# Moving 64 of 256 tokens out of the dense expert scans into gathers by index

## The chip, the core and the metric

The kernel runs on one core of a Trainium2 chip. The metric is the device time of one execution in microseconds. Work is done by TensorE (PE, with its weight loads shown as PEld), VectorE (DVE), ScalarE (ACT) and GpSimd (POOL); SyncE (SP) issues most transfers. Each engine works through its own queue in order and waits for the others by semaphores.

## The reference

The reference is a network of two layers of a first kind (three sequence mixers, then a routed feed-forward part) and two of a second kind (mixing, cross-attention, feed-forward), on 256 tokens of 1024 features. The change concerns the routed part, `peer_ffn`, which is computed once per layer of the first kind. For each token 8 heads pick 16 of 16384 experts each, by product keys:

```
q = (xt @ w_query).reshape(T, H, 2, PEER_HALF)
s = jnp.einsum('thcd,cnd->thcn', q, sub_keys)
sv, si = lax.top_k(s, K)
cand_s = (sv[:, :, 0, :, None] + sv[:, :, 1, None, :]).reshape(T, H, K * K)
cand_i = (si[:, :, 0, :, None] * PEER_NKEYS + si[:, :, 1, None, :]).reshape(T, H, K * K)
top_s, pos = lax.top_k(cand_s, K)
idx = jnp.take_along_axis(cand_i, pos, axis=-1)
gate = jax.nn.softmax(top_s, axis=-1)
a = jnp.einsum('thkd,td->thk', down[ib], xb)
c = gb * jax.nn.gelu(a)
out = jnp.einsum('thk,thkd->td', c, up[ib])
```

So a token needs 128 rows of `down` and 128 rows of `up`, each of 1024 values.

## The kernel before

`peer` does not gather. It computes the product of every token with every one of the 16384 experts, multiplies the result by a mask that holds the gate where the token picked the expert and zero elsewhere, and multiplies that by the whole `up` table. Both tables are read once per layer, in 128 tiles of 128 experts each (512 KB). There are four runs of 64 tiles, in this order: `dscan(0, ga[0])` (here the first down scan), `dscan(1, ga[1])` (the second down scan), `uscan(0)` (the first up scan) and `uscan(1)` (the second up scan).

Every weight tile goes through `wt` (line 248). SP loads it into one of four buffers `wr`; ACT rounds it to a high part `wh` (line 255), DVE subtracts that from the tile to get a low part `wl` (line 256), four buffers each. `mm3` (line 301) then does three products for each 128x128 piece: high by high (line 303), high by low (304), low by high (305), in the type fp32r, with new weights for each. A tile has 8 pieces, hence 24 products; the moving side is 128 features (or experts) by 256 tokens. In a down scan the products of two tiles are summed in PSUM (`col`) and ACT writes their GELU into `ga` (line 1179). In an up scan the moving side is the masked result, split into `xh` and `xl` by `coef` (line 1353, by way of lines 293 and 294), and all 256 experts' halves sum into four PSUM tiles `acc`.

Two helpers run beside the scans and put their instructions between the tiles. `routing()` picks the experts during the first down scan. `build(half, dst)` makes the masks, 8 tokens at a time: DVE writes one-hot rows (lines 1314 and 1329), PE multiplies them (line 1338, f16), DVE multiplies the mask into `ga` (line 1320). `build(0)` runs beside the second down scan and `build(1)` beside the first up scan, 32 blocks each.

How much of a helper stands between two tiles is set by credit. `tick` (line 267), called once by each `wt`, adds a rate to the credit (`R1` to `R3`: 1150, 1500, 1600) and takes steps of the helper as long as the credit is above zero; each step says its cost as it yields. `H1 = H2 = 0` ties the helper's DVE instructions behind the latest `wl`. `drain` runs a helper to its end. The second up scan has no helper.

Of the kernel before, what the change touches and what calls it, by code (L numbers as in the profile page):

```python
# [23 lines left out]
F32 = mybir.dt.float32  # L24
# [3 lines left out]
U32 = mybir.dt.uint32  # L28
AF = mybir.ActivationFunctionType
OP = mybir.AluOpType  # L30
# [90 lines left out]
def prep(inp):  # L121
# [11 lines left out]
    for l in range(DEPTH):  # L133
# [14 lines left out]
        a[f"sk{l}"] = bd  # L148
        a[f"down{l}"] = np.ascontiguousarray(
            i["peer_down"][l].reshape(128, 128, 8, 128).transpose(0, 3, 2, 1)).reshape(128, 128, 1024)  # L150
        a[f"up{l}"] = np.ascontiguousarray(i["peer_up"][l]).reshape(128, 128, 1024)

        w = i["w_in_2"][l]
# [44 lines left out]
class K:  # L198
    def __init__(self, ctx, tc, ap, ahead):
        self.tc, self.nc, self.ap, self.ctx = tc, tc.nc, ap, ctx  # L200
        nc = self.nc
        self.P = ctx.enter_context(tc.tile_pool(name="keep", bufs=1))
        self.W = ctx.enter_context(tc.tile_pool(name="wts", bufs=1))
        self.S = ctx.enter_context(tc.tile_pool(name="scr", bufs=1))
        self.ps = ctx.enter_context(tc.tile_pool(name="psum", bufs=1, space=PSUM))
        self.dr = ctx.enter_context(tc.tile_pool(name="dram", bufs=1, space=DRAM))
        self.x = self.P.tile([128, 8, T], F32, name="xres", bufs=1)
        self.nw = self.P.tile([128, 13, 8], F32, name="nw")
        self.eps = self.P.tile([128, 1], F32, name="eps")
# [20 lines left out]
        self.todo, self.sqs = [], []  # L230

    def cap(self, name, rows=128):
        o, w = _COFF[name]
# [31 lines left out]


    def tick(self):
        self.credit += self.rate
        while self.side is not None and self.credit > 0:
            try:  # L270
                cost = next(self.side)
                if cost is None:
                    break
                self.credit -= cost
            except StopIteration:
                self.side = None
        if self.side is None:
            self.credit = 0.0
# [131 lines left out]
    def tail(self, accs, rows, wi, scale=None):  # L410

        self.pre(wi)
        if wi == N_FIN:
# [5 lines left out]
        def done(d):  # L419
            s = slice(2 * d, 2 * d + 2)  # L420
            xs = self.x[:, s]
            if scale is None:
# [11 lines left out]
        self.lastrows(accs, rows, done)  # L434
        if wi != N_FIN:
            self.todo = self.norm_steps()
            return
# [38 lines left out]
    def colpair(self, srcs, xh, xl):  # L476
# [4 lines left out]
        else:  # L481
            for j, s in enumerate(srcs):
                h, l = self.wt(s)
                self.coltile(ps[:, j], h, l, xh, xl)
        return ps

    def cols(self, W, c0, n, xh, xl, evac):
# [625 lines left out]
WARM = 14  # L1113
R1, R2, R3 = 1150, 1500, 1600
H1 = H2 = 0


def peer(k, l, nxt):
# [4 lines left out]
    with k.tc.tile_pool(name=f"peer_{l}", bufs=1) as p:  # L1123
# [5 lines left out]
        ga1 = p.tile([128, HI * T], F32, name="ga1")  # L1129
        top = ExitStack()  # L1130
        q = top.enter_context(k.tc.tile_pool(name=f"first_{l}", bufs=1))
        ga = [q.tile([128, HI * T], F32, name="ga0"), ga1]

        rt, off = ga[1], [HI * T - 13000]

        def rtile(*shape):
            n = 1
# [1 line left out]
                n *= s  # L1139
            a = rt[:, off[0]:off[0] + n]  # L1140
            off[0] += n
            assert off[0] <= HI * T
# [12 lines left out]
        nc.sync.dma_start(sk, ap[f"sk{l}"])  # L1155
        k.cols(ap[f"w_q{l}"], 0, 8, xh, xl, lambda j, m, ps: V.tensor_mul(qT[:, j:j + m], ps, k.rsb))

        for h in range(0, 8, 2):
            for tt in range(2):
                ps = k.pst("mx", [128, 2, 256])  # L1160
                for j in range(2):
                    nc.tensor.matmul(ps[:, j], qT[:, h + j, tt * 128:(tt + 1) * 128], sk, start=True, stop=True)  # L1162
                c = h + tt
                t = k.S.tile([128, 2, T], F32, name="sq", bufs=2)[:, 0]
                V.scalar_tensor_tensor(t, k.x[:, c], k.nw[:, N_FFN + l, c:c + 1], k.rs, op0=OP.mult, op1=OP.mult)
                k.split(xh[:, c], xl[:, c], t)
                nc.scalar.copy(sc[:, tt, h:h + 2], ps)
        TB = 8
        room = k.P.tile([128, 4096], F16, name="xres", bufs=1)
        sizes = (TB * 128, TB * HI, 2 * TB * HI)  # L1170
# [5 lines left out]

        def dscan(half, dst):
            def ev(j, m, ps):
                nc.scalar.activation(dst[:, j * T:(j + m) * T], ps[:, :m].rearrange("p a t -> p (a t)"), AF.Gelu_apprx_tanh)  # L1179
            k.cols(down, half * HI, HI, xh, xl, ev)  # L1180


        sv = rtile(2, 8, 2, 16)
# [14 lines left out]
        def routing():  # L1198
# [79 lines left out]
            for src, kind in ((ij[0], 0), (ij[1], 1), (gt, 2)):  # L1278
# [8 lines left out]
                else:  # L1287
# [3 lines left out]
                    V.tensor_copy(g3[:, :, 0], gb)  # L1291
                    V.tensor_sub(g3[:, :, 1], gb, g3[:, :, 0])

        k.beside(routing(), R1, H1)
        dscan(0, ga[0])

        sets = [[room[:, starts[i]:starts[i + 1]] for i in range(3)],
                [k.S.tile([128, sizes[0]], F16, name="sq", bufs=2), room[:, starts[3] + sizes[0]:starts[3] + sizes[0] + sizes[1]],
# [1 line left out]
        pairs = io16.rearrange("p (a d) -> p a d", d=2)  # L1300

        def build(half, dst):
            d3 = dst.rearrange("p (i t) -> p i t", t=T)
            hs = slice(half * HI, (half + 1) * HI)

            def parts(b):
# [37 lines left out]
        dscan(1, ga[1])  # L1344
        k.drain()
        accs = k.rows_begin()
        ring = [k.S.tile([128, 8, T], F32R, name=n, bufs=1) for n in ("xh", "xl")]
        end = []

        def at(i):  # L1350
            return [t[:, i % 8] for t in ring] if i < 2 * HI - 2 else [t[:, i % 2] for t in end]

        def coef(i):
            r, o = i % 8, i % HI * T
            h, lo = [t[:, r:r + 2] for t in ring] if i < 2 * HI - 2 else end
            k.split(h.rearrange("p a t -> p (a t)"), lo.rearrange("p a t -> p (a t)"), ga[i // HI][:, o:o + 2 * T])

        def uscan(half):
            for i in range(half * HI, (half + 1) * HI, 2):
# [2 lines left out]
                if i % HI + 2 < HI:  # L1362
                    coef(i + 2)
                if i == 2 * HI - 2:
                    k.tail(accs, [k.wt(ap[f"up{l}"][e]) + tuple(at(e)) for e in (i, i + 1)], nxt, scale=1.0 / GS)
# [399 lines left out]
```

## Time and profile before

| | us |
|---|---|
| three runs, median | 2915.08 |
| lowest and highest of them | 2913.3, 2918.97 |
| the profiled execution | 2919.18 |
| its span | 2917.1 |
| PE busy in it | 2889.8 |
| DVE busy | 2077.0 |
| ACT busy | 1457.7 |

The span runs from the first to the last instruction of the profiled execution. An engine's busy time is the time in which at least one of its instructions was under way; PE's includes the run-out of pipelined products, so what a product costs is read from the distance between two starts.

### The profile page before, as it was taken

The numbers are of one execution on the slowest core, as the hardware profiler recorded it, in microseconds if no ns is written. First come the engines' busy times: TensorE is split into PE (matmuls) and PEld (weight loads), VectorE is DVE, ScalarE is ACT, GpSimd is POOL, SyncE is SP. The second block draws the span as 40 slices with busy tenths as digits, with TensorE's granted clock in tenths as the row PEclk, the third lists the DMA queues.
The fourth block names the chain that finished last, engine by engine and source line by source line (L and its number), as shares of the span: only waits on it lengthen the run. The fifth ranks groups of instructions, "written<-read, shape, count | busy, mean of one in ns | idle before, by whom it ended". The sixth has DMA issues, their size and how long they took to land.

```text
span 2917.1 us, 59823 instructions
## 1 busy us (share of the span) xinstructions
PE 2889.8 (99%) x25130; PEld 2836.1 (97%) x25130; DVE 2077.0 (71%) x3484; ACT 1457.7 (50%) x1963; POOL 0.2 (0%) x4
## 2 busy tenths in 40 slices
PE   9999999999999999999999999999999999999998
PEld 8989999999999989999999999999999999999998
DVE  7769978769755586798786895556667656667655
ACT  7655553443444476545434434444546544546544
POOL 0000000000000000000000000000000000000000
PEclk9999999999999999999999999999999999999999
DMA  6655554554555555555545445555455555455553
GB/s 202 182 171 168 182 179 163 166 171 160 188 181 184 179 171 181 176 178 184 169 163 172 163 160 195 182 184 189 153 173 188 179 183 179 162 186 181 174 182 129
DMA packets 150493, 511.50 MB, mean 175 GB/s; under 512 B 17176, under 2 KB 26520, under 8 KB 149200
## 3 DMA queue, kind: packets, MB, share of 16 engines
q1 hardware_dynamic: 145904, 503.02, 53.2%
q10 hardware_dynamic: 4320, 4.67, 0.5%
q8 instruction: 196, 3.21, 0.5%
q14 instruction: 73, 0.60, 0.1%
HBM read 500.23 MB, written 7.39 MB: 174 GB/s over the span
## 4 chain that ended last, share of the span: by engine, by line
PE 95%; ACT 2%; DMA 1%; DVE 1%; issue 0%; SPq 0%; ACTq 0%; DVEq 0%
PE col L303 18%; PE col L305 18%; PE col L304 18%; PE acc L303 12%; PE acc L304 12%; PE acc L305 12%; PE mx L1338 2%; ACT wh L255 1%; PE mx L1162 1%; DMA wr<-in_w_hi 0%; PE acc L658 0%; PE acc L1402 0%; DVE wl L256 0%; PE mx L341 0%; DMA c_tri<-in_consts 0%
## 5 line engine op out<-in xcount | busy, mean ns | idle before, releaser
L255 ACT CAST wh<-wr 128x1024 fp32r<-128x1024 f32 (+1 forms) x922 | 960.3, 1044 | 1276.0 <-PE col L304 594.5
L256 DVE TENSOR_TENSOR wl<-wr,wh 128x1024 fp32r<-128x1024 f32 (+1 forms) x922 | 1120.4, 1217 | 608.1 <-ACT wh L255 605.4
L303 PE MATMUL col<-xh,wh 128*128 128x256 f32 x3856 | 1104.7, 286 | 2.3 <-ACT silg L1574 0.9
L305 PE MATMUL col<-xh,wl 128*128 128x256 f32 x3856 | 1096.1, 284 | 4.6 <-DVE wl L256 4.6
L304 PE MATMUL col<-xl,wh 128*128 128x256 f32 x3856 | 1094.7, 284 | 0.0
L305 PEld LDWEIGHTS col<-xh,wl 128*128 128x128 f32 x3856 | 741.7, 192 | 6.8 <-DVE wl L256 5.4
L303 PEld LDWEIGHTS col<-xh,wh 128*128 128x128 f32 x3856 | 742.0, 192 | 4.5 <-ACT silg L1574 1.7
L304 PEld LDWEIGHTS col<-xl,wh 128*128 128x128 f32 x3856 | 742.0, 192 | 0.1
L303 PE MATMUL acc<-xh,wh 128*128 128x256 f32 x2016 | 574.4, 285 | 2.1 <-ACT xh L293 2.1
L304 PE MATMUL acc<-xl,wh 128*128 128x256 f32 x2016 | 570.5, 283 | 0.0
L305 PE MATMUL acc<-xh,wl 128*128 128x256 f32 x2016 | 570.1, 283 | 0.0
L303 PEld LDWEIGHTS acc<-xh,wh 128*128 128x128 f32 x2016 | 386.4, 192 | 2.4 <-ACT xh L293 2.4
L304 PEld LDWEIGHTS acc<-xl,wh 128*128 128x128 f32 x2016 | 387.1, 192 | 0.0
L305 PEld LDWEIGHTS acc<-xh,wl 128*128 128x128 f32 x2016 | 386.9, 192 | 0.0
L1320 DVE TENSOR_TENSOR ga<-ga,mx 128x512 f32<-128x512 f32 x128 | 87.3, 685 | 41.5 <-PE mx L1338 39.5
L304 PE MATMUL acc<-fl,wh 128*128 128x256 f32 x352 | 98.1, 279 | 0.0
L305 PE MATMUL acc<-fh,wl 128*128 128x256 f32 x352 | 98.0, 279 | 0.0
L303 PE MATMUL acc<-fh,wh 128*128 128x256 f32 x352 | 97.7, 280 | 0.0
L294 DVE TENSOR_TENSOR xl<-ga,xh 128x512 fp32r<-128x512 f32 x126 | 85.7, 683 | 0.0
L293 ACT CAST xh<-ga 128x512 fp32r<-128x512 f32 x126 | 76.9, 615 | 0.0
L1179 ACT ACTIVATE ga<-col 128x512 f32<-128x512 f32 x128 | 75.7, 592 | 0.0
L303 PE MATMUL col<-wh,xh 128*128 128x512 f32 (+3 forms) x192 | 70.7, 372 | 3.4 <-ACT hg L1076 2.0
(466 smaller groups left out, 3420.0 us busy)
## 6 DMA issues: line engine op xcount, KB each, us to landing
wr<-in_down SPq DMA_DIRECT2D x256, 512.0 KB, 3.5
wr<-in_up SPq DMA_DIRECT2D x256, 512.0 KB, 3.9
wr<-in_w SPq DMA_DIRECT2D x132, 512.0 KB, 3.9
wr<-in_w_in SPq DMA_DIRECT2D x106, 512.0 KB, 4.0
wr<-in_xa_k SPq DMA_DIRECT2D x16, 512.0 KB, 4.0
wr<-in_xa_v SPq DMA_DIRECT2D x16, 512.0 KB, 4.3
wr<-in_w_out SPq DMA_DIRECT2D x16, 512.0 KB, 3.4
wr<-in_w_q SPq DMA_DIRECT2D x16, 512.0 KB, 3.5
```

What stands on the lines that cost most here:

```text
L255: nc.scalar.copy(h[:, :w], r[:, :w])
L256: self.lows.append(nc.vector.tensor_sub(l[:, :w], r[:, :w], h[:, :w].bitcast(F32)).ins.name)
L293: self.nc.scalar.copy(h, src)
L294: self.nc.vector.tensor_sub(l, src, h.bitcast(F32))
L303: mm(ps, ah, bh, start=first, stop=False, skip_group_check=True)
L304: mm(ps, ah, bl, start=False, stop=False, skip_group_check=True)
L305: mm(ps, al, bh, start=False, stop=last, skip_group_check=True)
L1162: nc.tensor.matmul(ps[:, j], qT[:, h + j, tt * 128:(tt + 1) * 128], sk, start=True, stop=True)
L1179: nc.scalar.activation(dst[:, j * T:(j + m) * T], ps[:, :m].rearrange("p a t -> p (a t)"), AF.Gelu_apprx_tanh)
L1320: V.tensor_mul(dv, dv, ps.rearrange("p t i -> p i t"))
L1338: nc.tensor.matmul(ps[:, t], oj[:, t], gi[:, t, q], start=q == 0, stop=q == 1, skip_group_check=True)
```

## The change

64 tokens (the last ones, `GN`) leave the scans, and the other 192 (`TD`) stay in them. Every product of the scans has 192 columns instead of 256, `build` has 24 blocks instead of 32, and `ga`, `xh` and `xl` are narrower.

For the 64 tokens, the two halves of the 128 partitions hold the same tokens with different experts (`RS = 2`), so 64 steps (`NG`) cover a token's 128 experts. At the end of `routing` the expert numbers are formed and brought to that layout with two products (`gix`, `gga`). `gathered()` then runs as a second helper (`other`) beside the last three scans: POOL issues an indirect transfer of 128 rows (512 KB) into one of four buffers `grow`; DVE multiplies a row by the token's x and sums it (`tensor_tensor_reduce`), 64 times; GELU and gate follow for every 16; then 64 times DVE adds the coefficient times a row of `up` to `gacc` (`scalar_tensor_tensor`). At the end eight products with `gsel` put the sums of both halves into the last 64 columns of `acc`. The helper's rates are `GR2, GR3, GR4` (600, 500, 3000) for the three scans, and a step costs 1200. The host passes `peer_down` in its own row order as well (`rows{l}`).

```diff
     def tick(self):
+        if self.other is not None:
+            self.lent += self.orate
+            while self.other is not None and self.lent > 0:
+                c = next(self.other, None)
+                if c is None:
+                    self.other, self.lent = None, 0.0
+                else:
+                    self.lent -= c
         self.credit += self.rate
...
+GN = 64
+TD = T - GN
+RS = 128 // GN
+NG = 128 // RS
+NB = 4
+PSH = 0
+GR2, GR3, GR4 = 600, 500, 3000
...
-                k.split(xh[:, c], xl[:, c], t)
+                k.split(xh[:, c, :TD], xl[:, c, :TD], t[:, :TD])
+                nc.scalar.copy(t2[:, :128].rearrange("p (s t) -> p s t", s=RS), t[:, None, TD:].to_broadcast([128, RS, GN]))
+                nc.tensor.matmul(px[c // 4][:, c % 4 * 128:c % 4 * 128 + 128], t2[:, :128], k.ident, start=True, stop=True,
+                                 skip_group_check=True)
...
-            k.cols(down, half * HI, HI, xh, xl, ev)
+            k.cols(down, half * HI, HI, xh[:, :, :TD], xl[:, :, :TD], ev)
...
+            for n in range(NB - 1):
+                get(n)
+            for g in range(NG):
+                get(g + NB - 1)
+                r = rows.pop(0)
+                V.tensor_tensor_reduce(r, r, xg, 1.0, 0.0, OP.mult, OP.add, gav[:, g:g + 1])
+                if g % 16 == 15:
+                    s = slice(g - 15, g + 1)
+                    nc.scalar.activation(gav[:, s], gav[:, s], AF.Gelu_apprx_tanh)
+                    V.tensor_mul(gav[:, s], gav[:, s], gga[:, s])
+                yield 1200
+            V.memset(gacc, 0.0)
+            for g in range(NG):
+                get(NG + g + NB - 1)
+                r = rows.pop(0)
+                c = gav[:, g:g + 1]
...
+                    V.scalar_tensor_tensor(gacc, r, c, gacc, op0=OP.mult, op1=OP.add)
+                    yield 1200
+
+        k.other, k.orate = gathered(), GR2
...
-            n = T // TB
+            n = TD // TB
...
+            for j in range(2):
+                nc.tensor.matmul(accs[d][:, j, TD:], gacc[:, (2 * d + j) * 128:(2 * d + j + 1) * 128], gsel,
+                                 start=True, stop=True, skip_group_check=True)
...
-                        k.row(accs, *k.wt(ap[f"up{l}"][e]), *at(e), e == 0, False)
+                        k.row(part, *k.wt(ap[f"up{l}"][e]), *at(e), e == 0, False)
...
+        k.orate = GR3
         uscan(0)
...
+        k.orate = GR4
         uscan(1)
```

In `get`, which the steps call, the transfer is `nc.gpsimd.indirect_dma_start(out=r, in_=tabs[n // NG], in_offset=...gix[:, n % NG:n % NG + 1]...)`, with `tabs` the rows of `down` and of `up`.

DVE's queue in the second down scan, a stretch with mask blocks, in the kernel before (`wl` is the low part of a weight tile, `io16` with `rstd` or `jS` gives the one-hot rows, `ga0` the products that the mask goes into, `mx` the mask in PSUM):

```order
L256 TENSOR_TENSOR wl_5571<-wr_5568,wh_5570 128x1024
L1314 TENSOR_TENSOR xres_2637<-io16_2291,rstd_2638 128x512
L256 TENSOR_TENSOR wl_5621<-wr_5618,wh_5620 128x1024
L1314 TENSOR_TENSOR xres_2637<-io16_2291,rstd_2638 128x512
L1320 TENSOR_TENSOR ga0_2297<-ga0_2297,mx_5523 128x64x8
L1314 TENSOR_TENSOR xres_2637<-io16_2291,jS_2292 128x1024
L1329 TENSOR_TENSOR xres_2637<-xres_2637 128x1024
L256 TENSOR_TENSOR wl_5656<-wr_5653,wh_5655 128x1024
```

The same queue at such a place in the changed kernel, whose lines are numbered on by some tens (`grow` is a gathered row per partition, `xg` the tokens' x, `gav` the sums; the second row of a reduce step writes the sum out):

```order
L1366 ISA grow_5165,gav_2298<-grow_5165,xg_2294 128x1024
L1366 ISA gav_2298 128x1
L258 TENSOR_TENSOR wl_5495<-wr_5492,wh_5494 128x1024
L1404 TENSOR_TENSOR xres_2663<-io16_2291,rstd_2664 128x512
L1410 TENSOR_TENSOR ga0_2303<-ga0_2303,mx_5393 128x64x8
L1404 TENSOR_TENSOR sq_4974<-io16_2291,jS_2292 128x1024
L1419 TENSOR_TENSOR sq_4975<-xres_2663 128x1024
L258 TENSOR_TENSOR wl_5547<-wr_5544,wh_5546 128x1024
L1366 ISA grow_5253,gav_2298<-grow_5253,xg_2294 128x1024
```

A reduce step now stands between the subtractions, one to two tiles, and the mask work around it is what it was.

DVE's queue in the second up scan before (`xl` is the low part of the masked products of two tiles):

```order
L256 TENSOR_TENSOR wl_10335<-wr_10332,wh_10334 128x1024
L256 TENSOR_TENSOR wl_10365<-wr_10362,wh_10364 128x1024
L294 TENSOR_TENSOR xl_7601<-ga1_2293,xh_7600 128x512
L256 TENSOR_TENSOR wl_10397<-wr_10394,wh_10396 128x1024
L256 TENSOR_TENSOR wl_10427<-wr_10424,wh_10426 128x1024
```

And now, in the front part of that scan (`gacc` is the sum over the rows of `up`):

```order
L258 TENSOR_TENSOR wl_10512<-wr_10509,wh_10511 128x1024
L1382 SCALAR_TENSOR_TENSOR gacc_2295<-grow_10476,gav_2298,gacc_2295 128x1024
L304 TENSOR_TENSOR xl_7575<-ga1_2293,xh_7574 128x2x192
L1382 SCALAR_TENSOR_TENSOR gacc_2295<-grow_10479,gav_2298,gacc_2295 128x1024
L258 TENSOR_TENSOR wl_10550<-wr_10547,wh_10549 128x1024
L1382 SCALAR_TENSOR_TENSOR gacc_2295<-grow_10482,gav_2298,gacc_2295 128x1024
L1382 SCALAR_TENSOR_TENSOR gacc_2295<-grow_10515,gav_2298,gacc_2295 128x1024
L1382 SCALAR_TENSOR_TENSOR gacc_2295<-grow_10518,gav_2298,gacc_2295 128x1024
L258 TENSOR_TENSOR wl_10589<-wr_10586,wh_10588 128x1024
```

Two and three steps by turns stand between two subtractions. Of a layer's 128 steps 32 are in the queue in the second down scan, 27 in the first up scan, and 69 in the first 28 tiles of the second up scan.

## Rows read from the trace of the kernel before

**Rows 1.** The page: span, and busy time, share and instructions of each engine.
```profile
span 2917.1 us, 59823 instructions
PE 2889.8 (99%) x25130; PEld 2836.1 (97%) x25130; DVE 2077.0 (71%) x3484; ACT 1457.7 (50%) x1963; POOL 0.2 (0%) x4
```
**Rows 2.** The view of stretches, the four scans of layer 0: busy time per engine.
```profile
core 0: us, PE busy (x) PEld busy (x) DVE busy (x) ACT busy (x) POOL busy (x), PEclk, DMA share, GB/s
245.00:337.00 92.00, 92.00 (x769) 92.00 (x769) 88.37 (x354) 42.64 (x50) 0.00 (x0) 1.00 0.57 184
337.00:384.00 47.00, 47.00 (x394) 47.00 (x393) 40.27 (x84) 28.70 (x30) 0.00 (x0) 1.00 0.58 184
384.00:429.00 45.00, 45.00 (x378) 45.00 (x377) 30.85 (x39) 22.17 (x26) 0.00 (x0) 1.00 0.57 183
429.00:561.60 132.60, 132.60 (x1449) 131.31 (x1449) 111.16 (x157) 52.97 (x62) 0.00 (x0) 1.00 0.49 160
561.60:626.00 64.40, 64.40 (x579) 64.31 (x578) 32.87 (x34) 27.96 (x33) 0.00 (x0) 1.00 0.57 181
626.00:829.00 203.00, 201.93 (x2037) 200.56 (x2034) 163.41 (x221) 86.16 (x102) 0.00 (x0) 1.00 0.53 172
829.00:1014.00 185.00, 185.00 (x1545) 185.00 (x1544) 98.53 (x101) 83.66 (x99) 0.00 (x0) 1.00 0.58 185
```
**Rows 3.** PE in order of time, first down scan: start, duration, instruction.
```profile
249.99 0.28 PE L303 MATMUL col<-xh,wh 128*128 128x256 f32 x1
250.11 0.28 PE L304 MATMUL col<-xl,wh 128*128 128x256 f32 x1
```
**Rows 4.** PE in order of time, an earlier projection with 384 moving columns.
```profile
115.38 0.34 PE L305 MATMUL col<-wh,xl 128*128 128x384 f32 x1
...
115.90 0.33 PE L305 MATMUL col<-wh,xl 128*128 128x384 f32 x1
```
**Rows 5.** PE and its weight loads in order of time, plain f32, 64 columns.
```profile
88.27 1.10 PE L697 MATMUL acc<-hi,h_at 128*128 128x64 f32 x8
88.38 0.97 PEld L697 LDWEIGHTS acc<-hi,h_at 128*128 128x128 f32 x8
```
**Rows 6.** Weight loads grouped by line: count, busy us, mean ns of one, idle.
```profile
L303 PEld LDWEIGHTS col<-xh,wh 128*128 128x128 f32 x3856 | 742.0, 192 | 4.5 <-ACT silg L1574 1.7 <-ACT dt L1083 0.9 <-ACT wh L255 0.8
L1338 PEld LDWEIGHTS <-sq 128*128 128x128 f16 x1024 | 33.5, 98 | 2.5
L697 PEld LDWEIGHTS acc<-hi,h_at 128*128 128x128 f32 x32 | 4.2, 192 | 0.1
```
**Rows 7.** DVE grouped by line and shape.
```profile
L256 DVE TENSOR_TENSOR wl<-wr,wh 128x1024 fp32r<-128x1024 f32 x906 | 1105.2, 1222 | 603.0 <-ACT wh L255 600.6
...
L294 DVE TENSOR_TENSOR xl<-ga,xh 128x512 fp32r<-128x512 f32 x126 | 85.7, 683 | 0.0
...
L745 DVE SCALAR_TENSOR_TENSOR m_y<-xbc,small,m_y 128x256 f32<-128x256 f32 x42 | 18.9, 476 | 0.0
```
**Rows 8.** DVE in order of time, second down scan.
```profile
450.39 1.23 DVE L256 TENSOR_TENSOR wl<-wr,wh 128x1024 fp32r<-128x1024 f32 x1 [0.89 <-ACT wh L255]
451.53 0.42 DVE L1314 TENSOR_TENSOR xres<-io,rstd 128x512 f16<-128x512 f16 x1
```
**Rows 9.** The view of stretches, five us in the cross-attention part.
```profile
2205.00:2210.00 5.00, 5.00 (x45) 5.00 (x44) 5.00 (x11) 4.77 (x10) 0.00 (x0) 1.00 0.94 381
```
**Rows 10.** Transfers by issue: count, size, median us to landing.
```profile
wr<-in_up SPq DMA_DIRECT2D x256, 512.0 KB, 3.9
...
xres<-xd SPq DMA_DIRECT2D x2, 1024.0 KB, 7.7
```
**Rows 11.** PE grouped by line and shape, plain f32 products of 256 columns.
```profile
L1162 PE MATMUL mx<-ga 128*128 128x256 f32 x64 | 15.2, 387 | 0.0
```

More of the change, by code (lines that the diff above doesn't have):

```diff
@@ L230, in __init__ @@
         self.todo, self.sqs = [], []
+        self.other, self.orate, self.lent = None, 0.0, 0.0
     def cap(self, name, rows=128):
@@ L408, in lastrows, with tail @@
             done(d)
-    def tail(self, accs, rows, wi, scale=None):
+    def tail(self, accs, rows, wi, scale=None, part=None, more=None):
         self.pre(wi)
@@ L421, in done @@
             xs = self.x[:, s]
+            if more is not None:
+                more(d)
             if scale is None:
@@ L432, in done @@
             self.pre_pair(d)
-        self.lastrows(accs, rows, done)
+        self.lastrows(part or accs, rows, done)
         if wi != N_FIN:
@@ L1156, in peer @@
         k.cols(ap[f"w_q{l}"], 0, 8, xh, xl, lambda j, m, ps: V.tensor_mul(qT[:, j:j + m], ps, k.rsb))
+        px = [k.pst("acc") for _ in range(2)]
         for h in range(0, 8, 2):
@@ L1163, in peer @@
                 c = h + tt
-                t = k.S.tile([128, 2, T], F32, name="sq", bufs=2)[:, 0]
+                t2 = k.S.tile([128, 2, T], F32, name="sq", bufs=2)
+                t, t2 = t2[:, 0], t2[:, 1]
                 V.scalar_tensor_tensor(t, k.x[:, c], k.nw[:, N_FFN + l, c:c + 1], k.rs, op0=OP.mult, op1=OP.mult)
-                k.split(xh[:, c], xl[:, c], t)
+                k.split(xh[:, c, :TD], xl[:, c, :TD], t[:, :TD])
+                nc.scalar.copy(t2[:, :128].rearrange("p (s t) -> p s t", s=RS), t[:, None, TD:].to_broadcast([128, RS, GN]))
+                nc.tensor.matmul(px[c // 4][:, c % 4 * 128:c % 4 * 128 + 128], t2[:, :128], k.ident, start=True, stop=True,
+                                 skip_group_check=True)
                 nc.scalar.copy(sc[:, tt, h:h + 2], ps)
+        for i in range(2):
+            nc.scalar.copy(xg[:, 512 * i:512 * i + 512], px[i])
         TB = 8
@@ L1292, in routing @@
                     V.tensor_sub(g3[:, :, 1], gb, g3[:, :, 0])
+            pick = rtile(128)
+            nc.scalar.copy(pick.rearrange("p (s t) -> p s t", s=RS), k.ident[:, None, 128 - GN:].to_broadcast([128, RS, GN]))
+            V.scalar_tensor_tensor(ij[1][:, 1], ij[0][:, 1], 128.0, ij[1][:, 1], op0=OP.mult, op1=OP.add)
+            ps = k.pst("mx")
+            for i, src in enumerate((ij[1], gt)):
+                nc.tensor.matmul(ps[:, i * 128:i * 128 + 128], pick, src[:, 1].rearrange("p h k -> p (h k)"),
+                                 start=True, stop=True, skip_group_check=True)
@@ L1294, in peer @@
+            for s in range(RS):
+                pr = slice(s * GN, s * GN + GN)
+                pv = ps[pr].rearrange("p (c g s) -> p c g s", g=NG, s=RS)
+                V.tensor_copy(gix[pr], pv[:, 0, :, s])
+                nc.scalar.mul(gga[pr], pv[:, 1, :, s], GS)
+            yield 1000
+        V.tensor_add(gsel, k.ident[:, 0:GN], k.ident[:, GN:2 * GN])
+        for s in range(2, RS):
+            V.tensor_add(gsel, gsel, k.ident[:, s * GN:s * GN + GN])
         k.beside(routing(), R1, H1)
@@ L1295, in peer, with gathered, get @@
         dscan(0, ga[0])
+        k.drain()
+        def gathered():
+            tabs = [ap[f"rows{l}"], ap[f"up{l}"].rearrange("a b c -> (a b) c")]
+            rows = []
+            def get(n):
+                if n < 2 * NG:
+                    r = p.tile([128, D], F32, name="grow", bufs=NB)
+                    nc.gpsimd.indirect_dma_start(out=r, out_offset=None, in_=tabs[n // NG],
+                                                 in_offset=bass.IndirectOffsetOnAxis(ap=gix[:, n % NG:n % NG + 1], axis=0))
+                    rows.append(r)
+            for n in range(NB - 1):
[14 more added lines that the diff above has]
+                c = gav[:, g:g + 1]
+                if PSH and g % PSH[1] < PSH[0]:
+                    nc.scalar.mul(r, r, c)
+                    nc.gpsimd.tensor_add(pacc, pacc, r)
+                    yield 400
+                else:
+                    V.scalar_tensor_tensor(gacc, r, c, gacc, op0=OP.mult, op1=OP.add)
+                    yield 1200
@@ L1346, in peer, with more @@
         accs = k.rows_begin()
+        part = [a[:, :, :TD] for a in accs]
+        def more(d):
+            if d == 0:
+                while k.other is not None:
+                    k.lent = 1e9
+                    k.tick()
+            for j in range(2):
+                nc.tensor.matmul(accs[d][:, j, TD:], gacc[:, (2 * d + j) * 128:(2 * d + j + 1) * 128], gsel,
+                                 start=True, stop=True, skip_group_check=True)
         ring = [k.S.tile([128, 8, T], F32R, name=n, bufs=1) for n in ("xh", "xl")]
@@ L1364, in uscan @@
                 if i == 2 * HI - 2:
-                    k.tail(accs, [k.wt(ap[f"up{l}"][e]) + tuple(at(e)) for e in (i, i + 1)], nxt, scale=1.0 / GS)
+                    k.tail(accs, [k.wt(ap[f"up{l}"][e]) + tuple(at(e)) for e in (i, i + 1)], nxt, scale=1.0 / GS,
+                           part=part, more=more)
                 else:
                     for e in (i, i + 1):
-                        k.row(accs, *k.wt(ap[f"up{l}"][e]), *at(e), e == 0, False)
+                        k.row(part, *k.wt(ap[f"up{l}"][e]), *at(e), e == 0, False)
         k.beside(build(1, ga[1]), R3, H2)
+        k.orate = GR3
         uscan(0)
```

28 lines of the change are left out of this document (18 added, 10 removed).

## The prediction, made before the changed kernel was run

> **What bounds the kernel now.** I read the page first: PE is busy for 2889.8 of the 2917.1 us of the span [rows 1], so a change pays only if PE has less to do, and costs wherever PE is made to wait. The changed stage is the expert scans, 256 tiles of 512 KB per layer in four runs of 64 (first and second down scan, first and second up scan). So next I cut layer 0 into these stretches [rows 2]. PE is full in each: 245 to 429, 429 to 626, 626 to 829, 829 to 1014 us, that is 184, 197, 203 and 185 us. What differs is DVE, the engine that gets the new work: 88.4 of 92.0 us in the first half of the first down scan, 111.2 of 132.6 while the second down scan shares it with the mask building, about half in the second up scan. The slack that the change must live on is small in three of the four scans.
>
> A tile is 24 products. The starts of two of them stand 0.12 us apart at 256 columns [rows 3], so a tile costs 24 x 0.12 = 2.88 us, and 64 tiles 184 us. Where the masks are built, four tiles and three mask blocks take 13.2 us, 3.3 us a tile (132.6 us for 40.2 tiles).
>
> **PE: what 192 columns are worth.** At 384 columns the starts stand 0.173 us apart [rows 4], at 256 0.120: 0.053 us for 128 columns, which continued to 192 gives 0.093 us, or 2.24 us a tile. But each product also loads 128x128 new weights. The plain f32 products of line 697 have only 64 columns, and eight of their loads take 0.97 us of which the last is 0.192: (0.97 - 0.19)/7 = 0.111 us from one to the next [rows 5]. The loads of the scans last the same 0.192 us, those of the f16 mask products 0.098 [rows 6]. So I take 0.111 us as the floor of a product with a new 4-byte weight tile: 24 x 0.111 = 2.66 us a tile. PE saves 0.22 us a tile, 8%, not 25%. Bounds: 2.24 below, 2.88 (nothing won) above; 2.66 has the nearest row.
>
> [...]
>
> **DVE: what is added.** Per layer 64 multiply-and-reduce steps and 64 multiply-and-add steps over 128x1024 f32, each waiting in DVE's queue for its gathered rows. The nearest row is the low-part subtraction of a weight tile, 1.22 us [rows 7], 1.14 us from its start to the next one's [rows 8]. A step with a scalar costs 0.48 us at 256 elements [rows 7]; I add 0.06 to the 1.22 and, since each adds into the result of the one before, nothing of it overlaps: 1.3 us. The reduce step carries a second small instruction: 1.3 too. Bounds 1.14 and 1.5.
>
> [...]
>
> **Scan by scan, one layer.**
> First down scan. No gathers. DVE needs 88.4 us for the first 32 tiles, more than PE's 85; then PE's 2.66 us bind: 16.3 tiles 43.4, 15.6 tiles 41.6. Sum 173.4 against 184: -11.
>
> Second down scan. A tile's share of DVE in the mask stretch is 111.2/40.2 = 2.77 us; there are 24 blocks instead of 32, still three to four tiles, so 32 tiles. The order has one reduce step to two tiles, +0.65: 3.42 us. PE's own need is 2.66 + 0.42 (the mask products, 3.30 - 2.88 now) = 3.08, so DVE binds: 32 x 3.42 = 109. The other 32 tiles need 32.9/22.4 + 0.65 = 2.1 of DVE and go at PE's 2.66: 85. Sum 194 against 197: -2 or -3. I take -2.
>
> First up scan. Again 32 tiles with masks: 2.77 + 0.23 (the low part of two tiles' coefficients, 0.68 us [rows 7], a quarter shorter, the half of it less some overlap) + 0.42 x 1.3 = 3.54 us of DVE, 113 us; 32 tiles at 2.66, 85. 198 to 199 against 203: -4.
>
> Second up scan. Of 128 steps 32 + 27 are done, 69 are left, and they are issued at 2.5 to a tile. DVE: 1.14 + 0.23 + 2.5 x 1.3 = 4.62 us against PE's 2.66, for 69/2.5 = 27.7 tiles: 128 us. The low parts for PE stand in the same queue behind those steps, so PE waits. The other 36.3 tiles at 2.66: 97; 2 us tail. 227 against 185: +42. DVE sat idle for half of this scan before, but the steps use that idle time at its front only, and the back of the scan has PE's pace again.
>
> Transfers there: 0.52 + 2.5 x 0.52 = 1.83 MB a tile, at 4.62 us 397 GB/s. The fullest stretch of the trace has 381 GB/s at 0.94 of the engines [rows 9], 405 at all of them, 4.5 us a tile: the DMA engines are full too. Four row buffers turn in 4 x 1.85 = 7.4 us, so a gather has some 6 us to land before DVE waits. 512 KB land in 3.9 us now, 1 MB in 7.7 [rows 10]. At 7.7 a step would take (7.7 + 1.3)/4 = 2.25 us, 0.4 more, 28 us a layer; at 3.9 nothing. A gather issued by POOL is in no row. I take a quarter of it, +7.
>
> The rest: eight transposes of x, two index products, eight products that bring the sums back, each two passes of 0.11 us, with their copies: +4.
>
> Sum: -11 - 2 - 4 + 42 + 7 + 4 = +36 a layer, +72 for two. The profiled run took 2919.18 us (2.1 beside its span), 0.14% above the median of the runs, 2915.08. On the median: 2987; I say **2985 us**. Its own range is 2945 (steps at 1.2, gathers never late) to 3050 (products keep 0.12 us: +11, +7, +7, +8 a layer in the four scans).
>
> **Rivals.**
> *Columns set the pace.* If a product takes 0.093 us and weights load behind it, a tile is 2.24 us. First down scan 88.4 + 40.3 + 35 = 164 (-20), second 109 + 72 (-16), first up 113 + 72 (-18), second up 128 + 7 + 81 + 2 (+33), rest +4: -17 a layer, 2881 us, faster. It decides once a product takes under about 0.099 us (0.018 us less are worth 53 us a layer, and 36 are to be made good). For it: the starts fall evenly from 384 to 256 columns [rows 3, 4]. Against it: no 4-byte load in the rows follows another in under 0.111 us [rows 5]; the f16 products that do better have loads half as long [rows 6].
>
> *Gathers come one after another.* [...] If one lands only when the one before has, at 3.9 us [rows 10], the 69 steps take 269 instead of 135 us: +134 a layer, 3255; half of that effect gives 3120. Against it: plain loads do overlap in the full stretch [rows 9]. [...]
>
> *Narrow products cost as plain f32.* No product of this kind under 256 columns is in the trace. The plain f32 ones take 15.2 us for 64 records, two to a product [rows 11]: 0.475 us at 256 columns, 0.36 at 192. Then 8.6 us a tile, 512 x 5.7 = 2.9 ms more. Nothing but the gap in the rows speaks for it.
>
> **How the numbers follow.** Forecast 0.64, columns 0.16, serial gathers 0.15, plain f32 0.05. The range of 2865 to 3150 holds the forecast, most of the second case and the milder half of the third. What a measurement tells from no change is about 0.2%, 2909 to 2921: faster 0.17 (the second case and a sliver of the first), same 0.04, slower 0.79.
>
> **What would show it.** In the scans, starts of products 0.11 us apart: right; 0.093 or 0.12: the PE term is wrong. In the front 28 tiles of the second up scan PE should stand idle for some 40%, ended by the low-part subtraction, with DVE near full and the DMA engines above 0.9; behind them PE is full again. If DVE waits there for the gathers, the third case is at work. [...] If the first three scans end later than before, the steps cost more than 1.3 us or the products did not get shorter.

## The result and the profile after

The changed kernel takes 3014.55 us (median of four runs, 3008.45 to 3016.39) against 2914.4 for the kernel before on the same chip (2913.3 to 2918.97): a ratio of 1.0337, 95% interval 1.0318 to 1.0356. It is slower, by 100 us; 72 were forecast. The profiled execution took 3013.12 us.

The page of the kernel after answers to [rows 1]: 15 us less work on PE, 211 more on DVE, and a span that is 94 longer.

```profile
span 3011.2 us, 59942 instructions
PE 2874.6 (95%) x24690; PEld 2811.2 (93%) x24690; DVE 2287.8 (76%) x3758; ACT 1439.4 (48%) x2000; POOL 308.6 (10%) x260
```

The view of stretches of the kernel after, layer 0, answers to [rows 2]: the first down, second down and first up scan, then the front and the back of the second up scan.

```profile
core 0: us, PE busy (x) PEld busy (x) DVE busy (x) ACT busy (x) POOL busy (x), PEclk, DMA share, GB/s
239.00:420.00 181.00, 175.51 (x1545) 174.82 (x1545) 159.90 (x497) 89.77 (x106) 6.70 (x5) 0.98 0.62 190
420.00:608.00 188.00, 186.12 (x1954) 185.47 (x1953) 165.75 (x229) 81.38 (x101) 33.49 (x32) 1.00 0.83 274
608.00:803.00 195.00, 187.49 (x1886) 186.29 (x1887) 172.34 (x248) 79.69 (x99) 31.44 (x28) 0.98 0.77 249
803.00:965.00 162.00, 125.20 (x776) 121.59 (x775) 129.75 (x120) 41.32 (x51) 81.41 (x63) 0.76 0.89 315
965.00:1051.00 86.00, 86.00 (x773) 86.00 (x771) 46.13 (x48) 39.00 (x47) 0.00 (x0) 1.00 0.68 196
```

Three scans are shorter and one is much longer. The stretch from 803 to 965 us holds the first 28 tiles of the second up scan, the front, and some four tiles more. No engine is busy all the time there: PE 125 of 162 us, DVE 130, the DMA engines 0.89. The granted clock (the share of its full speed that TensorE was given), 1.00 in every stretch of [rows 2], is 0.76 there. The front by itself, 149.7 us:

```profile
803.20:952.90 149.70, 112.91 (x674) 109.29 (x674) 122.85 (x114) 36.05 (x44) 81.41 (x63) 0.74 0.91 321
```

Measured from the first product of one scan to the first of the next (the last scan: to the start of its last high-by-high product), the scans of layer 0 last, in us ("front" is the first 28 tiles of the second up scan; the last column is the time of the whole kernel):

| kernel | first down | second down | first up | second up | front | time, median |
|---|---|---|---|---|---|---|
| before | 190.7 | 204.1 | 200.9 | 183.9 | 80.6 | 2914.4 |
| after | 181.4 | 188.1 | 195.1 | 248.2 | 149.7 | 3014.55 |
| scans alone | 181.1 | 186.6 | 184.1 | 172.5 | 75.0 | 2833.69 |
| steps even in the last scan | 181.3 | 188.2 | 193.6 | 185.5 | 78.8 | 2882.4 |
| no gathers | 181.3 | 192.1 | 191.7 | 217.6 | 120.0 | 2958.12 |
| no steps | 181.3 | 186.6 | 184.1 | 231.0 | 132.4 | 2958.16 |
| filled pauses | 181.3 | 188.2 | 195.4 | 246.7 | 148.7 | 3005.27 |
| five row buffers | 181.3 | 188.2 | 193.6 | 229.2 | 131.6 | 2968.28 |
| steps spread | 181.4 | 186.6 | 184.4 | 172.5 | 75.0 | 2835.28 |
| 32 tokens out | 181.9 | 195.0 | 201.5 | 172.5 | 75.0 | 2883.91 |

The 190.7 us of the kernel before are not all the scan's own. In its queue on PE, 24 of the 32 records of the plain f32 products of line 1162, which belong to the part ahead, stand behind the scan's first product, and hold it up by 5.6 us. In the kernels after, all of them stand ahead of it. To compare like with like, the first down scan before is 185.1 us.

PE in order of time, kernel after (start, duration): products of 192 columns start 0.11 us apart, where [rows 3] has 0.12.

```profile
449.77 0.27 PE L313 MATMUL col<-xh,wh 128*128 128x192 f32 x1
449.88 0.27 PE L314 MATMUL col<-xl,wh 128*128 128x192 f32 x1
```

DVE grouped by line and shape, kernel after; it answers to [rows 7]. The two kinds of step last 1284 ns and 1222 plus 87 ns.

```profile
L258 DVE TENSOR_TENSOR wl<-wr,wh 128x1024 fp32r<-128x1024 f32 x906 | 1104.8, 1223 | 459.4 <-ACT wh L257 457.6 <-issue 0.9
L1382 DVE SCALAR_TENSOR_TENSOR gacc<-grow,gav,gacc 128x1024 f32<-128x1024 f32 x128 | 164.4, 1284 | 57.1 <-DMA grow<-in_up,gix 53.7 <-issue 1.5
L1366 DVE CUSTOM_DVE_ANT_0 grow<-grow,xg 128x1024 f32<-128x1024 f32 x128 | 156.2, 1222 | 1.5 <-DMA grow<-in_rows,gix 1.5
...
L1366 DVE DVE_READ_ACCUMULATOR2_ANT gav<- 128x1 f32 x128 | 11.1, 87 | 0.0
```

The waits between 803 and 965 us, kernel after (who waited for whom: us, times, longest). Weight tiles and gathered rows land late, and PE waits for the low part that stands in DVE's queue behind them.

```profile
ACT wh L257 <- DMA wr<-in_up: 80.6, 19, 6.5
POOL grow L1357 <- DVE gacc L1382: 47.2, 36, 4.2
PEld acc L315 <- DVE wl L258: 40.3, 19, 4.1
PE acc L315 <- DVE wl L258: 36.8, 17, 3.9
ACT wh L257 <- PE acc L314: 30.9, 9, 5.9
DVE gacc L1382 <- DMA grow<-in_up,gix: 24.3, 29, 1.9
...
DVE wl L258 <- ACT wh L257: 5.4, 5, 2.0
```

DVE in order of time in that stretch: a step stalls for its row (in brackets), and the next weight subtraction stalls with it.

```profile
865.47 2.61 DVE L1382 SCALAR_TENSOR_TENSOR gacc<-grow,gav,gacc 128x1024 f32<-128x1024 f32 x2 [0.83 <-DMA grow<-in_up,gix]
867.99 1.22 DVE L258 TENSOR_TENSOR wl<-wr,wh 128x1024 fp32r<-128x1024 f32 x1
870.67 1.29 DVE L1382 SCALAR_TENSOR_TENSOR gacc<-grow,gav,gacc 128x1024 f32<-128x1024 f32 x1 [1.46 <-DMA grow<-in_up,gix]
```

### The profile page after: what moved, and what is told of

Same layout as the page of the kernel before. It is cut to its first block, busy times and chain, and to the rows that moved or that the text cites. A ratio compares the mean times of both kernels' runs of the same rounds, so it can differ in the third digit from the quotient of the medians.

```text
span 3011.2 us, 59942 instructions
## 1 busy us (share of the span) xinstructions
PE 2874.6 (95%) x24690; PEld 2811.2 (93%) x24690; DVE 2287.8 (76%) x3758; ACT 1439.4 (48%) x2000; POOL 308.6 (10%) x260
## 4 chain that ended last, share of the span: by engine, by line
PE 57%; issue 23%; DMA 8%; POOL 5%; DVE 4%; ACT 3%; POOLq 0%; SPq 0%; ACTq 0%; DVEq 0%
PE col L313 12%; PE col L315 12%; PE col L314 12%; DMA grow<-in_up,gix 7%; PE acc L313 5%; PE acc L315 5%; PE acc L314 5%; POOL grow L1357 5%; DVE wl L258 1%; ACT wh L257 1%; DVE gacc L1382 1%; PE mx L1188 0%; PE acc L670 0%; PE acc L1506 0%; PE mx L351 0%
## 5 line engine op out<-in xcount | busy, mean ns | idle before, releaser
L313 PE MATMUL col<-xh,wh 128*128 128x192 f32 (+1 forms) x3856 | 1088.5, 282 | 14.8 <-ACT ga L1211 10.9
L315 PE MATMUL col<-xh,wl 128*128 128x192 f32 (+1 forms) x3856 | 1081.1, 280 | 3.3 <-DVE wl L258 3.3
L314 PE MATMUL col<-xl,wh 128*128 128x192 f32 (+1 forms) x3856 | 1080.1, 280 | 1.2 <-DVE xl L309 1.2
L315 PE MATMUL acc<-xh,wl 128*128 128x192 f32 x2016 | 590.5, 293 | 77.2 <-DVE wl L258 77.0
L313 PE MATMUL acc<-xh,wh 128*128 128x192 f32 x2016 | 587.6, 292 | 1.7 <-ACT xh L303 1.7
L314 PE MATMUL acc<-xl,wh 128*128 128x192 f32 x2016 | 585.6, 291 | 3.4 <-DVE xl L304 3.4
L1357 POOL DMA_INDIRECT grow<-in_rows,gix x128 | 141.3, 1104 | 1558.4 <-DVE xres L1325 911.9
L1382 DVE SCALAR_TENSOR_TENSOR gacc<-grow,gav,gacc 128x1024 f32<-128x1024 f32 x128 | 164.4, 1284 | 57.1 <-DMA grow<-in_up,gix 53.7
L1357 POOL DMA_INDIRECT grow<-in_up,gix x128 | 167.1, 1305 | 121.8 <-DVE gacc L1382 97.5
L1366 DVE CUSTOM_DVE_ANT_0 grow<-grow,xg 128x1024 f32<-128x1024 f32 x128 | 156.2, 1222 | 1.5 <-DMA grow<-in_rows,gix 1.5
```

The source lines that it names most:

```text
L313: mm(ps, ah, bh, start=first, stop=False, skip_group_check=True)
L314: mm(ps, ah, bl, start=False, stop=False, skip_group_check=True)
L315: mm(ps, al, bh, start=False, stop=last, skip_group_check=True)
L1357: nc.gpsimd.indirect_dma_start(out=r, out_offset=None, in_=tabs[n // NG], in_offset=bass.IndirectOffsetOnAxis(ap=gix[:, n % NG:n % NG + 1] ...
L1366: V.tensor_tensor_reduce(r, r, xg, 1.0, 0.0, OP.mult, OP.add, gav[:, g:g + 1])
L1382: V.scalar_tensor_tensor(gacc, r, c, gacc, op0=OP.mult, op1=OP.add)
```

## The experiments

Three theories of the long front were open: VectorE's sum of work (A), the DMA engines (B) and the granted clock (C).

**Steps even in the last scan.** One number differs:

```diff
-GR2, GR3, GR4 = 600, 500, 3000
+GR2, GR3, GR4 = 600, 500, 1400
```

> The changed kernel with one number altered: in the second up scan the row steps come at 1400 instead of 3000 a weight tile, 1.17 steps a tile over nearly the whole scan instead of 2.5 over its front half. Work, transfers and sums are the same. Three theories of the second up scan, which takes about 242 us after the change against 185 before. A, VectorE's sum: 69 steps of 1.29 us and 64 tiles of 1.41 us are 179 us, 63 less in each layer: about 2890 us. B, the DMA engines: 64 weight tiles and 69 gathers of 0.524 MB are 70 MB, at the 0.33 MB/us that the crowded stretch reaches 212 us, 30 less in each layer: about 2955 us, with a DMA share near 0.9 over the whole scan. C, TensorE's granted clock, which is 0.76 in that stretch after TensorE has paused for VectorE: without long pauses it stays at 1.00 and the scan takes TensorE's 172 to 180 us, about 2885 us.

Measured: 2882.4 us, 0.987 of before (0.9853 to 0.9887). More than the whole loss of the change came from where the 69 steps of the last scan stood. The scan takes 185.5 us, near the sum of A (179). C had said much the same (172 to 180 us, about 2885 in all), so this run does not decide between A and C. B as I had put it is wrong: the view of stretches of this kernel shows the DMA engines at 384 GB/s, not 330, with PE's clock at 1.00.

```profile
860.00:920.00 60.00, 56.19 (x487) 54.80 (x486) 57.19 (x56) 26.16 (x31) 36.99 (x24) 1.00 1.01 384
```

**No gathers, and no steps.** In the one, `get` hands out four fixed buffers; in the other each step works on one column:

```diff
-                    r = p.tile([128, D], F32, name="grow", bufs=NB)
-                    nc.gpsimd.indirect_dma_start(...)
-                    rows.append(r)
+                    rows.append(fixed[n % NB])
```
```diff
-                    V.scalar_tensor_tensor(gacc, r, c, gacc, op0=OP.mult, op1=OP.add)
+                    V.scalar_tensor_tensor(gacc[:, :1], r[:, :1], c, gacc[:, :1], op0=OP.mult, op1=OP.add)
```

> All 128 gathers of a layer are left out; the 128 VectorE steps stay where they are and read four row buffers that are set to zero once, so the 64 tokens' expert output is not computed. A: VectorE sets the pace of the front (2.5 steps of 1.29 us and 1.41 us for the weight tile are 4.62 us), so the second up scan hardly changes: 128 us for its front and 97 us for its rest are 225 us against 242, which is less than a per cent: 2980 to 3014 us. B: the DMA engines made the front longer than that sum, so the scan falls from 242 us to the 225 us of VectorE's sum, and weight tiles no longer come late: 2975 us, and the wait of the cast for weight tiles (68 us in layer 0's front) is gone. C: the clock falls all the same, since TensorE still pauses for VectorE, and with 24 products of 0.213 us a tile cannot be under 5.1 us: 5.1 x 27.7 + 97 = 238 us, 3005 us, granted clock in the front near 0.76 as now.

> All gathers stay, at the same places; each VectorE step of 1.22 to 1.28 us is replaced by one on a single element of the row per partition, so the 64 tokens' expert output is not computed. A: with the steps gone VectorE's work is 1.41 us a tile and the second up scan falls from 242 to TensorE's 172 us; the 59 steps in the two scans before it give back about 38 us more where VectorE was full: 3014 - 2 x 108 = about 2800 us. B: the front stays at its DMA pace (1.83 MB a tile at 0.33 MB/us, 5.56 us a tile, 28 tiles) and only the two scans before gain: about 2940 us, DMA share at or above 0.9 in the front and TensorE waiting there for late weight tiles. C: the clock would show it, as it falls where TensorE has paused: below 1.00 if B holds, 1.00 if A does.

Measured: 2958.12 us (ratio 1.0138, 1.0121 to 1.0155) and 2958.16 us (1.0141, 1.0124 to 1.0158). Neither A nor B alone accounts for the front: DVE's work by itself makes the front 120 us long, the transfers by themselves 132, both together 150. The stretches show which one is full in each: DVE 63.6 of 65 us without gathers, the DMA engines 0.97 without steps.

```profile
805.00:870.00 65.00, 50.62 (x375) 48.91 (x375) 63.64 (x61) 21.02 (x26) 0.00 (x0) 0.89 0.38 115
```
```profile
830.00:875.00 45.00, 33.77 (x227) 32.51 (x226) 16.68 (x35) 10.15 (x13) 25.30 (x22) 0.83 0.97 356
```

PE pauses in both, and the clock falls with it, to 0.89 and 0.83.

**Scans alone.** Neither gathers nor steps (`V.memset(gacc, 0.0)` in place of the second helper).

> The narrower scans alone: 64 tokens leave the four expert scans of each layer, with no gather and no step, so their expert output is left out. What the narrowing is worth. With weight loads of 4-byte values setting 0.111 us a product, a tile of 24 products takes 2.68 us and a scan 172 us, with VectorE below that in the mask tiles too (3.1 us there after the change less half a step of 1.29 us is 2.45 us): four scans take about 696 us against about 799 after and 769 before: 3014 - 2 x 103 = about 2808 us. If the mask tiles stay bound by VectorE, the second down and first up scans stay near 180 us and the time is near 2840 us. If columns set the pace (0.093 us a product), it would be below 2700 us.

Measured: 2833.69 us, 0.971 of before (0.9694 to 0.9727), near the second guess. The last scan is 64 x 2.695 = 172.5 us. The mask tiles of the second down scan are bound by PE itself, though, not by VectorE: the first row, its mask stretch, has PE busy throughout and DVE for 84 of 97 us. The second row is the last scan.

```profile
423.00:520.00 97.00, 97.00 (x1116) 96.78 (x1115) 84.24 (x120) 39.78 (x48) 0.00 (x0) 1.00 0.58 172
...
794.00:966.00 172.00, 172.00 (x1543) 172.00 (x1542) 92.84 (x96) 79.28 (x95) 0.00 (x0) 1.00 0.66 196
```

So the narrowing is worth 84 us, and the gathers and steps, as they were placed, cost 181.

**128 columns.** The same with `GN = 128`.

> As the narrower scans alone, but with 128 instead of 64 tokens out of the expert scans, so the expert output of 128 tokens is left out. Products have 128 columns instead of 192. If loads of 4-byte weights set the pace, products still start 0.111 us apart, the scan without a mask stays at 172.5 us, and only the mask gets shorter (16 instead of 24 groups of 16 small products, about 5 us less in each of two scans): about 2815 us against 2834. [...]

Measured: 3553 to 3873 us, where 2815 was the guess; the granted clock differs between its runs (0.77 on average in one, 0.70 in three), so its time is not compared. The floor of 0.111 us under a product shows all the same. PE in order of time, first in the first down scan, where the clock is still 1.00, then at 600 us, where it is 0.50:

```profile
310.08 0.27 PE L315 MATMUL col<-xh,wl 128*128 128x128 f32 x1
310.19 0.28 PE L313 MATMUL col<-xh,wh 128*128 128x128 f32 x1
...
600.12 0.41 PE L313 MATMUL col<-xh,wh 128*128 128x128 f32 x1
600.33 0.41 PE L314 MATMUL col<-xl,wh 128*128 128x128 f32 x1
```

At full clock products of 128 columns start 0.111 us apart (median of 491 between 245 and 300 us), the same as with 192. What I had not expected is in the stretches of this kernel: PE pauses for 3.1 us near 353 us, the clock falls to 0.50, and it stays there through the rest of the layer's scans although PE is busy throughout.

```profile
300.00:345.00 45.00, 45.00 (x405) 45.00 (x405) 43.73 (x175) 19.50 (x25) 0.00 (x0) 1.00 0.63 189
...
350.00:360.00 10.00, 6.93 (x44) 6.79 (x45) 5.42 (x8) 5.86 (x5) 0.00 (x0) 0.81 0.43 123
360.00:365.00 5.00, 5.00 (x26) 5.00 (x25) 2.04 (x3) 3.62 (x4) 0.00 (x0) 0.50 0.51 173
...
360.00:1480.00 1120.00, 1120.00 (x5625) 1119.86 (x5624) 371.94 (x445) 262.81 (x330) 0.00 (x0) 0.50 0.33 103
```

With 192 columns (the scans alone) PE pauses for 4.1 us at the same place, and from 365 us on the clock is back at 1.00:

```profile
360.00:365.00 5.00, 5.00 (x33) 5.00 (x32) 3.68 (x4) 1.57 (x2) 0.00 (x0) 0.66 0.59 165
365.00:370.00 5.00, 4.63 (x42) 4.46 (x41) 3.25 (x6) 4.28 (x6) 0.00 (x0) 1.00 0.28 91
```

**Filled pauses.** Ahead of each of the first 28 tiles' own products:

```diff
+                            for n in range(FILL):
+                                nc.tensor.matmul(f[:, :TD], h[:, n % 8 * 128:n % 8 * 128 + 128], at(e)[0],
+                                                 start=True, stop=True, skip_group_check=True)
```

> The changed kernel, with 16 extra products of 192 columns in each of the first 28 tiles of the second up scan, into a bank that nobody reads, placed ahead of the tile's own products: TensorE works where it paused for VectorE. A full-speed tile then holds 40 products x 0.1115 = 4.46 us, below both VectorE's sum (4.62, measured 4.7 without gathers) and the transfers' pace (4.9 without steps); now a tile takes 5.85 us there at a granted clock of 0.76. If the half clock after pauses is what lifts 5.85 over those two, the clock stays near 1.00 and the front falls towards 28 x 4.9 = 137 us, 25 less in each layer: about 2965 us. If the clock costs nothing (TensorE waits anyway), the clock rises and the time stays at 3014 us or above. If the clock falls although TensorE works, 40 products of 0.213 us are 8.5 us a tile: above 3100 us.

Measured: 3005.27 us (ratio 1.0305, 1.0285 to 1.0325, which overlaps that of the change). The clock is back at 0.95 and the front still takes 148.7 us, so the fallen clock is a trace of the waits and hardly a cost. The extra products are work too, so a small cost of the clock may be hidden behind them; theory C in the size that I had put it, 25 us a layer, is out. The first row is the kernel after, the second, from this run, has PE busy with the extra products.

```profile
830.00:895.00 65.00, 46.24 (x279) 44.64 (x278) 52.49 (x47) 15.04 (x18) 37.44 (x30) 0.75 0.93 329
```
```profile
830.00:895.00 65.00, 58.16 (x481) 57.04 (x480) 51.49 (x46) 15.07 (x18) 36.07 (x28) 0.95 0.92 326
```

**Five row buffers.** `NB = 5` in place of 4.

> The changed kernel with five row buffers for the gathers instead of four, so that a gather is asked for one step earlier. If gathers that land late, and hold up VectorE's queue with the weight subtractions behind them, are what puts the front of the second up scan (162 us) above VectorE's sum (130 us without gathers), about a third of that goes: 3014 - 2 x 10 = about 2994 us, and the 24 us that VectorE waits for rows in layer 0's front fall. If memory traffic or the clock is what counts, nothing changes: 3010 to 3018 us.

Measured: 2968.28 us (1.0178, 1.0161 to 1.0195), 46 us better than the change and more than twice what I expected. The front falls from 149.7 to 131.6 us, just what the transfers take by themselves, and VectorE's wait for rows between 803 and 965 us from 24.3 to 11.0 us. In the same stretch as above DVE is now busy for 59 instead of 52 us and the DMA engines move 375 instead of 329 GB/s:

```profile
830.00:895.00 65.00, 48.18 (x305) 46.38 (x304) 59.22 (x54) 17.44 (x21) 42.74 (x33) 0.80 0.99 375
```

So the last 18 us of the front were a coupling of the two: with four buffers a late row stops DVE, DVE then frees no row buffer, POOL waits (47.2 us in the waits above) and the DMA engines idle in their turn.

**Steps spread.** The second helper takes its rate by whether the mask building is at work:

```diff
-            self.lent += self.orate
+            self.lent += self.orate if self.side is None else self.busy
...
-GR2, GR3, GR4 = 600, 500, 3000
+GR2, GR3, GR4 = 1100, 1100, 1100
+GM2, GM3 = 400, 150
```

> All work of the changed kernel, with the row steps spread by where VectorE has room: few beside the mask building (400 and 150 instead of 600 and 500 a weight tile), 1100 a tile elsewhere in the last three scans: 16, 25, 4, 30 and 53 of the 128 steps fall in the mask part and the rest of the second down scan, the same of the first up scan, and the second up scan. By VectorE's sum (1.29 us a step, 1.14 to 1.41 a tile) every stretch then fits under TensorE's pace, and the time comes near that of the narrower scans alone, 2834 us: with 1 to 4 us lost in each of the three scans about 2850 us, against 2882 where only the second up scan was evened out. If the DMA engines are the limit (one gather and one weight tile in 2.7 us are 390 GB/s, the most seen is 384), the stretches without mask run at 2.8 us a tile: about 2870 us.

Measured: 2835.28 us, 0.972 of before (0.9704 to 0.9737): the best version, 15 us below the guess, and as fast as the scans with no gather at all. Its stretches: PE is busy to within 1 us in the last three scans, with DVE at 91 to 96% and the DMA engines at 360 GB/s in the last. The 384 GB/s of the run with even steps are not needed: 53 gathers and 64 tiles in 172.5 us are 61 MB, 356 GB/s.

```profile
421.00:608.00 187.00, 186.14 (x1958) 185.77 (x1957) 175.03 (x245) 81.75 (x102) 48.13 (x39) 1.00 0.85 295
608.00:792.00 184.00, 183.52 (x1886) 183.13 (x1886) 177.44 (x248) 80.09 (x100) 46.52 (x34) 1.00 0.78 276
792.00:965.00 173.00, 173.00 (x1552) 173.00 (x1551) 156.87 (x153) 80.32 (x97) 74.49 (x51) 1.00 0.96 360
```

**32 tokens out.** `GN = 32`, two row buffers, `GR4 = 600`.

> 32 instead of 64 tokens leave the scans, all of the work is done: products of 224 columns, 28 mask groups, 64 gathers and steps a layer instead of 128, at the rates of the changed kernel in the second down and first up scans (32 and 27 steps), the last 5 at 600 a tile. Two row buffers, since the tables of 224 columns need the room, and the sum shares its buffer with the tokens' x. Loads of 0.111 us cap both 128 and 192 columns; the line from 384 (0.173) over 256 (0.120) meets 0.111 near 234 columns. If the load sets the pace at 224 too, a tile is 2.68 us as with 64 tokens, the second up scan takes about 174 us without the step front, and the four scans about 181 + 189 + 195 + 174 = 739 us against 813 with 64 tokens and 780 before: about 2850 to 2865 us, half the gathers for the same gain on TensorE. If a product goes by its columns there (0.1155 us, halfway between 192 and 256), the scans take 25 us more a layer: about 2905 us. If two row buffers make VectorE wait for rows, the mask stretches lose a microsecond a step: above 2920 us.

Measured: 2883.91 us, 0.989 of before (0.9873 to 0.9906), between two of the guesses. The last scan is 172.5 us, exactly as with 192 columns: the floor sets the pace at 224 too, and the first guess holds there. The rest of the gain is lost in the mask stretches, which are longer with 28 groups (195.0 and 201.5 us), where DVE has no room for steps at these rates (the first row below, the mask stretch of the second down scan, has it busy for all of 106 us); rows are not what it waits for there (0.3 us).

```profile
424.00:530.00 106.00, 104.99 (x1215) 104.12 (x1214) 105.94 (x160) 43.28 (x53) 16.77 (x17) 1.00 0.77 247
```
```profile
900.05 0.28 PE L313 MATMUL acc<-xh,wh 128*128 128x224 f32 x1
900.16 0.27 PE L314 MATMUL acc<-xl,wh 128*128 128x224 f32 x1
```

## Why the prediction was right, and where it was off

**The product: right.** 0.111 us was read from eight plain loads [rows 5]; where PE does not pause and the clock is 1.00, the starts in the scans stand 0.112 us apart on average at 128, 192 and 224 columns alike. The first rival, columns as the pace, is out, and so is the third (plain f32 at 0.36). That it is the load, and not some other fixed cost of a product of 4-byte values, is likely but not shown: every such product here brings new weights. The f16 mask products, whose loads last 98 instead of 192 ns, start 0.03 us apart.

**The steps: right.** 1.3 us forecast; they last 1.28 and 1.31 us. The reduce step's 1.31 are 1222 and 87 ns. Work on POOL at the same time hardly shows on VectorE's side: weight subtractions that overlap a gather's instruction on POOL last 1224 ns, the others 1222. POOL's own instruction lasts 0.93 to 2.0 us; what makes the long ones was not looked into.

**The first three scans.** Forecast 173.4, 194 and 198 to 199 us; measured 181.4, 188.1 and 195.1. Against the kernel before (185.1, 204.1, 200.9) they gain 3.7, 16.0 and 5.8 us, where 11, 2 and 4 were forecast. Two of the three terms were mis-sized.

The first down scan goes at 2.68 us a tile from its start, a little faster than the 88.4 us that I gave its first 32 tiles, but PE pauses once for 4.1 us, near 352 us. It waits there for ACT's GELU (line 1211), which stands behind instructions of the routing that wait for DVE. The granted clock falls, and eight tiles take 29.3 instead of 21.4 us. The forecast had no such pause; the scans alone have it too.

```profile
352.00:360.00 8.00, 4.17 (x22) 4.00 (x21) 4.11 (x4) 5.18 (x5) 0.00 (x0) 0.64 0.46 152
```

In the second down scan I kept VectorE's 2.77 us a tile in the mask stretch, as if the mask blocks still stood as close, and so had VectorE bind at 3.42. In the kernel after, 33 mask tiles take 102 us, 3.1 each, with VectorE just full. The 17 steps among them take 20.9 us of its time, which leaves 2.45 a tile for the rest.

```profile
414.00:516.00 102.00, 100.93 (x1141) 100.60 (x1141) 101.89 (x154) 41.24 (x52) 17.76 (x16) 1.00 0.80 262
```

The time before, 197 us, was also too short by 7: the stretch from 429 to 626 us [rows 2] leaves out the scan's first 6 us and its last one. The forecast itself counted all 64 tiles.

**The second up scan: the mechanism right, its wait too small.** The front is slow because VectorE and the DMA engines are both nearly full, and PE waits for the low parts in VectorE's queue, as forecast. The forecast was 128 us for VectorE's sum and 7 for late gathers; the front took 149.7. The sum was set a little high: VectorE is busy for 122.9 us in the front, and without gathers the front lasts 120.0. The wait was set far too low: 7 us was a quarter of the worst case that I had worked out; DVE waits 24.3 us for rows. I had seen that VectorE and the DMA engines would both be nearly full (4.62 and 4.5 us a tile) and treated the longer one as the price. Two resources that are both nearly full, joined by four buffers, cost 150 us where they need 120 and 132. The scan is 64 us longer than before; +49 was forecast.

Of the signs, VectorE's full queue came out only in part: it is busy for 82% of the front, and PE stands idle for 25% instead of 40%. The granted clock, 1.00 in every stretch of [rows 2], fell to 0.74 in the front, where PE pauses. The scan is longer than VectorE's sum, but the filled pauses show that the clock is hardly the cause.

**The rest.** +4 a layer was forecast for the parts around the scans. Of the 94 us between the two spans the scans hold 39 in layer 0 and 41 in layer 1 (with 185.1 us for the first down scan before), so 14 lie outside. The scans alone have them too (17 us by the same count), so neither gathers nor steps are the cause. Most of the 14 lie right behind the two second up scans (4 and 7 us, by the starts of the same products). PE pauses longer there than before, and the clock falls: between 1057 and 1062 us it is busy for 2.5 of 5 us, and in the next 5 us the clock is 0.50. Why it pauses there was not taken apart.

**The sum.** The forecast of +32 us for the scans of a layer stands against +39 and +41. Behind it stand larger errors that offset each other: in layer 0 the first down scan gained 7 us less than said, the second down scan 14 more, the first up scan 2 more, and the second up scan lost 15 more. That the sum came so near is partly luck. Of the 28 us between the +72 that were forecast and the 100 between the medians, 16 lie in the scans, 6 outside, and 6 between the profiled runs (94 apart) and the medians. The lower end of the forecast's own range, 2945, does not follow from its two conditions: steps at 1.2 and gathers never late are worth 17 us a layer, which gives about 2951.

**The second rival**, gathers one after another, was the right place and the wrong mechanism. They are late by 24 us in a front, not 134, and a fifth buffer takes more than half of that back. With five buffers a gather of `up` lands 7.5 us after its issue (median of the 128), and in the front one is issued every 2.1 us: several are under way at once.

## What to carry to other kernels

Work that is moved to an engine with slack must be spread over the stretches where that slack is: the same 128 steps cost 181 us at one set of rates and nothing at another. Where two resources that share a few buffers would both take longer than the engine that they feed (in the front 4.3 and 4.7 us a tile against TensorE's 2.7), do not price the longer one alone: price the buffers between them, or slow both. Once both stayed just under TensorE's pace (0.91 and 0.96 in the last scan with the steps spread), nothing was lost. A product with a new 4-byte 128x128 weight tile has a floor of 0.111 us at full clock here, so narrowing its moving side from 224 columns to 192 bought nothing more. Before two kernels are compared stretch by stretch, see that the same instructions stand in each stretch: here 5.6 us of another part stood inside a scan before, and outside it after.

## What the runs showed of the hardware

- With products of 128 columns the granted clock fell to 0.50 after a pause of 3.1 us and stayed there with PE busy for 1120 us (0.213 us a product); with 192 columns it came back to 1.00 after one of 4.1 us. What decides this was not looked into.
- Gathers of 128 rows of 4 KB and plain weight loads together reach 384 GB/s, about as much as the 381 of plain loads alone in [rows 9]. POOL is busy for 1.1 us on average for a gather from `down`, and 1.3 for one from `up`, in the kernel after.
- Products with new 4-byte weights start 0.111 us apart at a clock of 1.00 and 0.213 at 0.50, whether they have 128 or 192 columns; f16 products of 64 columns with new weights start 0.03 us apart.
